# Hybrid decoder block on one core: x fetched ahead of the first scale block, column sums by products with ones, x turned a quarter at a time

## The chip, the core and the metric

The kernel runs on one core of a Trainium2 chip. The core has a matrix engine (TensorE, PE in the profile), a vector engine (VectorE, DVE), a scalar engine (ScalarE, ACT), a general engine (GpSimd, POOL) and a queue engine (SyncE, SP). All of them run their own instruction stream in order and wait for each other by semaphores; loads and stores are issued by SP, POOL and ACT and carried by 16 DMA engines. The metric is the device time of one execution in microseconds (us), the median of several runs.

## The reference

The input x has 512 positions by 2048 channels in float32. The part that matters here is the beginning:

```
mod = silu(c) @ w_ada + b_ada                     # c: 2048 values; w_ada: 2048 x 12288
shift1, scale1, gate1, shift2, scale2, gate2 = split(mod, 6)
h    = rms_norm(x, norm1_w) * (1 + scale1) + shift1
proj = h @ w_in                                   # w_in: 2048 x 7168, seven parts of 1024
attn = dilated_attention(q, k, v of proj)         # 8 heads
hg   = hgrn2(q, f, i, g of proj)                  # 8 heads of a gated recurrence
x    = x + gate1 * (concat(attn, hg) @ w_out)
x    = x + gate2 * (square(relu(h2 @ w_ff1)) @ w_ff2)   # h2: as h, with scale2 and shift2
```

Each sixth of mod needs 2048 x 2048 values of w_ada, 16.8 MB, to make 2048 numbers.

## The kernel before

Channels lie on the 128 partitions, 16 chunks k of 128 channels. The vector-matrix product for mod runs on VectorE: a block of columns of w_ada is loaded chunk by chunk (`araw`), and each chunk is multiplied by its 128 values of silu(c) and added to one of two running sums (`acc`, lines 127 and 129; one such instruction is called a multiply-add below). For scale1 a block has 256 columns: 8 loads of 256 KB and 16 multiply-adds. That gives the factors g1c of two chunks, so there are 8 scale blocks, and block p serves chunks 2p and 2p+1, called pair p. For shift1 and the others a block has 512 columns and 16 loads. The sums over the partitions are made by turning the sums on TensorE (`to_cols`, line 149) and adding along the row on ScalarE (line 152); two small VectorE operations (lines 167 and 169) add the bias and multiply by norm1_w.

x is loaded in 16 tiles `xs` (4 tiles of positions by 4 quarters of channels, line 255). ScalarE squares 14 of them and VectorE 2; the norm factor rx is ready after a power on GpSimd (line 212). The tiles are multiplied by rx (2 on ScalarE, 14 on VectorE, lines 277 and 279), turned on TensorE four at a time (line 283) and copied out (line 285), giving `xnT[k]`. For each chunk, `scaled` multiplies xnT[k] by g1c in place (line 335), rounds it into `hi` (line 336, ScalarE) and keeps the rest in `lo` (line 337, VectorE). Weights are treated likewise: `whi` (line 39, ScalarE) and `wlo` (line 40, VectorE), four buffers of each. A product is three TensorE products, hi by whi, lo by whi, hi by wlo.

`first_groups` (called once with scale1 alone, group 1, and once again, group 2) makes 512 + 256 columns of w_in: for each pair it takes 36 products of 128 x 512. The shift is added later, as a column made by another vector-matrix product (`shift_through`): its first one ends with an addition at line 143, is turned at line 149, and stands in TensorE's order inside the third projection, after 660 products of 128 x 512. The shift blocks, their columns and the first gate block are background steps (`bgw`), taken from within group 2.

The order of the instructions is set by a scheduler at build time, which puts them on each engine by its own estimate of when they can run; `issue_after` adds an order on one engine, and from the third projection on TensorE's order is the written one. At run time each engine follows its list. All loads of the first part stand in SP's list.

Of the kernel before, what the change touches and what calls it, by code (L numbers as in the profile page):

```python
# [15 lines left out]
P = 128  # L16
# [28 lines left out]
def hybrid_block(ctx, tc, x, c, positions, norm1_w, w_ada, b_ada, w_in, q_norm_w, k_norm_w,  # L45
# [29 lines left out]
    pool.memset(mhalf, -0.5)  # L75
# [10 lines left out]
    dve.tensor_copy(bcol, ps_c[:, 2 * NK:P])  # L86
    sc = const.tile([P, NK], F32, name="sc")
# [28 lines left out]
    def gemv(view, vec, col0, n=512, early=False):  # L116
# [3 lines left out]
        for k0 in range(0, NK, nk):  # L120
            raw = spare.pop(0) if early and spare else slot("araw") if early else gv.tile([P, 512], F32, name="araw", bufs=4)
            raw = raw.rearrange("p (k n) -> p k n", n=n)
            nc.sync.dma_start(raw, view[:, k0:k0 + nk, col0:col0 + n])
            for k in range(k0, k0 + nk):
                acc = accs[k % 2]
                if k < 2:
                    dve.tensor_scalar(acc, raw[:, k - k0], vec[:, k:k + 1], None, op0=ALU.mult)
                else:
                    dve.scalar_tensor_tensor(acc, raw[:, k - k0], vec[:, k:k + 1], acc, op0=ALU.mult, op1=ALU.add)  # L129
# [8 lines left out]
    def to_cols(accs, dst):  # L138

        nb = accs[0].shape[1] // P  # L140
        parts = 1 if nb == 4 else 2
        if parts == 1:
            dve.tensor_tensor(accs[0], accs[0], accs[1], op=ALU.add)
        yield
        pc = bank("pc")
        for j in range(nb):
            for u in range(parts):
                c = (j * parts + u) * P
                pe.transpose(pc[:, c:c + P], accs[u][:, j * P:(j + 1) * P], ident)
        for j in range(nb):  # L150
            c = pc[:, j * parts * P:(j + 1) * parts * P]
            act.activation(c, c, AF.Copy, accum_out=dst[:, j:j + 1])
# [7 lines left out]
    def mod_cols(kind, b, dst, nw, n=512, early=False):  # L160

        for _ in gemv(ada_v, sc, kind * D + b * n, n, early):
            yield
        nb = n // P
# [3 lines left out]
        if nw is not None:  # L168
            mod_cols.last = dve.scalar_tensor_tensor(d, d, 1.0, nw[:, b * nb:(b + 1) * nb], op0=ALU.add, op1=ALU.mult)
# [16 lines left out]
    def load_w(view, k0, c0, n=512, eng=None, ahead=True, raws=None):  # L186
        with tc.high_priority() if ahead else ExitStack():
            raw = wr.tile([P, 2, n], F32, name="wraw", tag="raw", bufs=4)
            nc.sync.dma_start(raw, view[:, k0:k0 + 2, c0:c0 + n])
# [20 lines left out]
    def rstd_of(dst, ss, n, inv_n):  # L210
        dve.tensor_scalar(dst, ss, inv_n, EPS, op0=ALU.mult, op1=ALU.add)
        pool.tensor_tensor(dst, dst, mhalf[:, 0:n], op=ALU.pow)
# [34 lines left out]
    first_scale = mod_cols(1, 0, g1c, n1c, 256, True)  # L247
    for _ in range(8):
        next(first_scale)
# [1170 lines left out]
```

## Time and profile before

| what | value |
|---|---|
| runs (median; all) | 2300.57 us; 2303.32, 2300.57, 2293.37 |
| the profiled execution | 2297.95 us, span in the profile 2296.2 us, mean granted TensorE clock 0.996 |
| busy in the span | PE 2224.9 us (97%), DVE 1809.9 (79%), ACT 1098.2 (48%), POOL 447.3 (19%) |
| first 128 x 512 product of the kernel | at 36.80 us |
| moved by DMA | 598.31 MB, mean 261 GB/s |

Times are counted from the start of the span. A row of the timeline has start, duration, engine, line, operation, out<-in with sizes, a count where equal instructions follow each other, and in brackets how long the engine had been idle and what ended it. The duration of an instruction includes its tail; where many follow each other, the pace is the distance of their starts, which is shorter. A row of the waits has who waited for whom, the total, the number of times and the longest. A row of the windows has, for a stretch, the busy time of PE, weight loads, DVE, ACT and POOL with counts, the granted clock, the DMA engines' share and GB/s.

### The profile page before, as it was taken

How to read it: one execution, taken by the hardware profiler on the slowest of the kernel's cores; microseconds unless marked ns; L12 is line 12 of the kernel's file. 1: busy time of each engine (PE TensorE's matmuls, PEld its weight loads, DVE VectorE, ACT ScalarE, POOL GpSimd, SP SyncE). 2: the span in 40 equal slices, each digit the busy share in tenths (PEclk: the TensorE clock that was granted, in tenths of full speed). 3: DMA queues.
4: the chain of work that ended last, by engine and by line, in shares of the span. 5: the costliest groups of instructions: out<-in, count | busy, mean ns of one | idle time of the engine just before them, and what ended most of it. 6: DMA issues, size and time to landing. Idle time of an engine off the chain costs nothing.

```text
span 2296.2 us, 33105 instructions
## 1 busy us (share of the span) xinstructions
PE 2224.9 (97%) x11769; PEld 1824.4 (79%) x11769; DVE 1809.9 (79%) x2765; ACT 1098.2 (48%) x1950; POOL 447.3 (19%) x664
## 2 busy tenths in 40 slices
PE   4899999999999999999999999999999999999999
PEld 3787877888778888778887888888888888888887
DVE  6999777677876565668648988988897679967878
ACT  5555434433344454447544556555564333343332
POOL 1000022000230000002232323323332222222221
PEclk9999999999999999999999999999999999999999
DMA  9798455556545256746969799889889987998784
GB/s 327 254 335 315 124 177 156 177 160 207 187 151 184 68 173 225 247 152 217 367 231 383 251 344 347 298 306 386 298 328 390 339 293 260 385 344 291 278 301 164
DMA packets 262582, 598.31 MB, mean 261 GB/s; under 512 B 23220, under 2 KB 43968, under 8 KB 262416
## 3 DMA queue, kind: packets, MB, share of 16 engines
q1 hardware_dynamic: 186800, 332.54, 43.1%
q0 software_dynamic: 70720, 254.21, 30.0%
q10 hardware_dynamic: 4896, 9.44, 1.2%
q8 instruction: 93, 1.52, 0.3%
q14 instruction: 73, 0.60, 0.1%
HBM read 518.49 MB, written 77.61 MB: 260 GB/s over the span
## 4 chain that ended last, share of the span: by engine, by line
PE 60%; DVE 17%; DMA 14%; issue 6%; ACT 2%; POOL 1%; SPq 0%; DVEq 0%; ACTq 0%; POOLq 0%
PE f L1177 9%; PE f L1178 9%; PE f L1176 9%; DMA araw<-in_w_ada_dram 6%; PE prj L198 5%; PE prj L199 5%; PE prj L200 5%; DVE vlo L1161 3%; DVE acc L129 3%; DVE raw L1144 2%; PE f L208 2%; PE f L206 2%; PE f L207 2%; DMA Fl<-f_lod 2%; DVE wlo L40 2%
## 5 line engine op out<-in xcount | busy, mean ns | idle before, releaser
L1160 ACT CAST vhi<-raw 128x1024 fp32r<-128x1024 f32 x392 | 413.4, 1055 | 534.5 <-PE f L1178 416.3
L1161 DVE TENSOR_TENSOR vlo<-raw,vhi 128x1024 fp32r<-128x1024 f32 x392 | 475.5, 1219 | 153.5 <-ACT vhi L1160 152.7
L1177 PE MATMUL f<-vlo,Fh 128*128 128x512 f32 x1376 | 537.1, 390 | 3.9 <-DVE vlo L1161 3.8
L1178 PE MATMUL f<-vhi,Fl 128*128 128x512 f32 x1376 | 535.8, 389 | 0.8 <-DMA Fl<-f_lod 0.8
L1176 PE MATMUL f<-vhi,Fh 128*128 128x512 f32 x1376 | 536.1, 390 | 0.0
L39 ACT CAST whi<-wraw 128x512 fp32r<-128x512 f32 (+1 forms) x368 | 219.8, 601 | 453.2 <-PE prj L200 313.3
L198 PE MATMUL prj<-whi,hi 128*128 128x512 f32 x896 | 364.9, 407 | 1.3 <-ACT gg L701 1.3
L200 PE MATMUL prj<-whi,lo 128*128 128x512 f32 x896 | 351.4, 392 | 0.0
L199 PE MATMUL prj<-wlo,hi 128*128 128x512 f32 x896 | 351.0, 392 | 0.0
L40 DVE TENSOR_TENSOR wlo<-wraw,whi 128x512 fp32r<-128x512 f32 (+1 forms) x368 | 243.2, 665 | 120.9 <-ACT whi L39 118.3
L129 DVE SCALAR_TENSOR_TENSOR acc<-araw,sc,acc 128x512 f32<-128x512 f32 (+1 forms) x392 | 252.7, 672 | 100.5 <-DMA araw<-in_w_ada_dram 99.2
L1177 PEld LDWEIGHTS f<-vlo,Fh 128*128 128x128 f32 x1376 | 258.3, 188 | 63.3 <-DVE vlo L1161 10.0
L1178 PEld LDWEIGHTS f<-vhi,Fl 128*128 128x128 f32 x1376 | 258.3, 188 | 54.8 <-DMA Fl<-f_lod 1.6
L1176 PEld LDWEIGHTS f<-vhi,Fh 128*128 128x128 f32 x1376 | 258.3, 188 | 53.5
L1144 DVE TENSOR_TENSOR raw<-raw,raw 128x1024 f32<-128x1024 f32 x224 | 267.7, 1216 | 4.1 <-DMA raw<-in_w_ff_dram 3.9
L198 PEld LDWEIGHTS prj<-whi,hi 128*128 128x128 f32 x896 | 169.3, 189 | 36.5 <-ACT gg L701 1.6
L200 PEld LDWEIGHTS prj<-whi,lo 128*128 128x128 f32 x896 | 168.9, 188 | 36.7
L199 PEld LDWEIGHTS prj<-wlo,hi 128*128 128x128 f32 x896 | 169.5, 189 | 33.0 <-DVE wlo L40 1.0
L1122 POOL DMA_DIRECT2D Fh<-f_hid x112 | 79.0, 705 | 425.9 <-PE f L1178 410.8
L208 PE MATMUL f<-hi,wlo 128*128 128x512 f32 x256 | 99.8, 390 | 1.3 <-DVE wlo L40 1.3
L206 PE MATMUL f<-hi,whi 128*128 128x512 f32 x256 | 100.2, 391 | 0.0
L207 PE MATMUL f<-lo,whi 128*128 128x512 f32 x256 | 99.6, 389 | 0.0
(311 smaller groups left out, 2917.0 us busy)
## 6 DMA issues: line engine op xcount, KB each, us to landing
raw<-in_w_ff_dram SPq DMA_DIRECT2D x224, 512.0 KB, 9.7
araw<-in_w_ada_dram SPq DMA_DIRECT2D x384, 256.0 KB, 4.3
Fh<-f_hid POOLq DMA_DIRECT2D x112, 512.0 KB, 6.5
Fl<-f_lod POOLq DMA_DIRECT2D x112, 512.0 KB, 7.7
wraw<-in_w_in_dram SPq DMA_DIRECT2D x104, 512.0 KB, 4.1
Fh<-h_hid POOLq DMA_DIRECT2D x60, 512.0 KB, 6.6
Fl<-h_lod POOLq DMA_DIRECT2D x60, 512.0 KB, 7.5
f_hid<-part POOLq DMA_DIRECT2D x48, 512.0 KB, 7.9
```

The lines of the kernel that those rows point to most:

```text
L39: nc.scalar.copy(hi, src)
L40: (eng or nc.vector).tensor_tensor(lo, src, hi.bitcast(F32), op=ALU.subtract)
L129: dve.scalar_tensor_tensor(acc, raw[:, k - k0], vec[:, k:k + 1], acc, op0=ALU.mult, op1=ALU.add)
L198: pe.matmul(banks[ti], lhsT=hi[:, ts], rhs=whi, start=first, stop=False)
L199: pe.matmul(banks[ti], lhsT=hi[:, ts], rhs=wlo, start=False, stop=False)
L200: pe.matmul(banks[ti], lhsT=lo[:, ts], rhs=whi, start=False, stop=last)
L1144: dve.tensor_tensor(dst, a, b, op=ALU.subtract)
L1160: act.copy(hi, src)
L1161: split_done.append(dve.tensor_tensor(lo, src, hi.bitcast(F32), op=ALU.subtract))
L1176: pe.matmul(banks[t], lhsT=fh[u][a][:, ts], rhs=whi[:, a], start=first, stop=False)
L1177: pe.matmul(banks[t], lhsT=fh[u][a][:, ts], rhs=wlo[:, a], start=False, stop=False)
L1178: pe.matmul(banks[t], lhsT=fl[u][a][:, ts], rhs=whi[:, a], start=False, stop=end)
```

## The change

Six things are changed, all before the third projection:

1. The 16 loads of x are issued first; the 8 loads of scale block 0 follow, then the first pair's weights, then the other 56 loads of the scale blocks in a row. Before, scale block 0 was ahead of x, and weights and scale loads alternated.
2. The weights of group 1 (from pair 1 on) and of group 2 are issued by POOL instead of SP.
3. The squares are shared 8 to 8 between ScalarE and VectorE (14 to 2 before), the multiplications by rx 8 to 8 (2 to 14 before).
4. A scale block's sums over the partitions are two products with a column of ones for each chunk (`L188` in the new file), and one ScalarE instruction applies norm1_w and a bias prepared at the start (`L191`). The turning, the adding along rows and the two VectorE operations go.
5. x is turned a quarter at a time: quarter 0 before scale block 0 is summed, each other quarter inside the loop over pairs. `scaled` makes hi first and the scaled xnT after it.
6. `behind` fixes the order of the steps on each engine: a block's multiply-adds come after the block ahead and, except the first four, after the last `lo` of the pair that this block's forerunner serves.

The instruction lists of the changed kernel differ as follows (order of issue only; no times). VectorE, around the place where scale block 2 ends and chunks 4 and 5 are split; acc is a running sum, wlo the rest of a weight tile, lo the rest of a chunk, g1c the scale factors. Before:

```order
L127 TENSOR_SCALAR acc<-araw,sc 128x256 x2
L129 SCALAR_TENSOR_TENSOR acc<-araw,sc,acc 128x256
L169 SCALAR_TENSOR_TENSOR g1c<-g1c,n1c 128x2
L129 SCALAR_TENSOR_TENSOR acc<-araw,sc,acc 128x256 x8
L337 TENSOR_TENSOR lo_687<-xnT,hi_686 128x512
L129 SCALAR_TENSOR_TENSOR acc<-araw,sc,acc 128x256 x2
L40 TENSOR_TENSOR wlo<-wraw,whi 128x512
```

Now:

```order
L133 SCALAR_TENSOR_TENSOR acc<-araw,sc,acc 128x256 x2
L40 TENSOR_TENSOR wlo<-wraw,whi 128x256
L133 SCALAR_TENSOR_TENSOR acc<-araw,sc,acc 128x256
L337 TENSOR_TENSOR lo_618<-xnT,hi_617 128x512
L337 TENSOR_TENSOR lo_623<-xnT,hi_622 128x512
L312 TENSOR_SCALAR xs<-xs,rx 128x512 x2
L131 TENSOR_SCALAR acc<-araw,sc 128x256 x2
L40 TENSOR_TENSOR wlo<-wraw,whi 128x512
L133 SCALAR_TENSOR_TENSOR acc<-araw,sc,acc 128x256 x2
L40 TENSOR_TENSOR wlo<-wraw,whi 128x512
```

Before, multiply-adds of the next block stand between the end of a block and the chunk's `lo`; now the chunk's `lo` follows directly on the block's last multiply-add, and the next block's come behind it.

ScalarE at the same place in the changed kernel (xnT copies are turned quarters of x on their way out of PSUM, hi the rounded chunks, whi the rounded weights):

```order
L320 COPY xnT<-ptx 128x512
L191 ACTIVATE g1c<-pc,bcol,n1c 128x1 x2
L335 ACTIVATE hi_617<-xnT,g1c 128x512
L320 COPY xnT<-ptx 128x512
L335 ACTIVATE hi_622<-xnT,g1c 128x512
L336 ACTIVATE xnT<-xnT,g1c 128x512
L320 COPY xnT<-ptx 128x512
L336 ACTIVATE xnT<-xnT,g1c 128x512
```

`lo_618` reads the first of the two L336 results, so five ScalarE instructions stand between the sums and it.

The diff, cut to its core:

```diff
+    ones = mhalf[:, 16:17]
...
+    b1c = bcol[:, NK:2 * NK]
+    dve.scalar_tensor_tensor(b1c, b1c, 1.0, n1c, op0=ALU.add, op1=ALU.mult)
...
-    def to_cols(accs, dst):
...
-        nb = accs[0].shape[1] // P
-        parts = 1 if nb == 4 else 2
...
+    def to_cols(accs, dst, lag=1):
+
+        dve.tensor_tensor(accs[0], accs[0], accs[1], op=ALU.add)
+        for _ in range(lag):
+            yield
         pc = bank("pc")
...
+    def scale_cols(b):
+
+        steps = gemv(ada_v, sc, D + b * 256, 256, True)
+        for _ in range(NK // 2):
+            with ExitStack() as order:
+                for ins in scale_cols.behind:
+                    order.enter_context(tc.issue_after(ins))
+                next(steps)
+            yield
+        next(steps, None)
+        scale_cols.behind = [gemv.last.ins, gemv.load.ins]
+        accs = gemv.acc
+        scale_cols.last_dve = gemv.last
+        pc = bank("pc")
+        for j in range(2):
+            for u in range(2):
+                pe.matmul(pc[:, j:j + 1], lhsT=accs[u][:, j * P:(j + 1) * P], rhs=ones, start=u == 0, stop=u == 1)
+        for j in range(2):
+            ks = slice(2 * b + j, 2 * b + j + 1)
+            scale_cols.last = act.activation(g1c[:, ks], pc[:, j:j + 1], AF.Identity, scale=n1c[:, ks],
+                                             bias=b1c[:, ks])
+        yield
...
-    first_scale = mod_cols(1, 0, g1c, n1c, 256, True)
-    for _ in range(8):
-        next(first_scale)
...
-                if q == 3 and ti % 2:
+                if ti % 2:
...
+    def x_turned(k, *anchors):
+
+        q, j = k // 4, k % 4
+        if j == 0:
+            for ti in range(NT):
+                if ti % 2:
+                    with tc.issue_after(anchors[0].ins):
+                        x_turned.dve = dve.tensor_scalar(xs[ti][q], xs[ti][q], rx[:, ti:ti + 1], None, op0=ALU.mult)
+                else:
+                    with tc.issue_after(anchors[1].ins):
+                        x_turned.act = act.activation(xs[ti][q], xs[ti][q], AF.Copy, scale=rx[:, ti:ti + 1])
+        pt = bank("ptx")
+        for ti in range(NT):
+            x_turned.pe = pe.transpose(pt[:, ti * P:(ti + 1) * P], xs[ti][q][:, j * P:(j + 1) * P], ident)
+        t = slot("xnT")
+        act.copy(t, pt)
+        xnT.append(t)
...
+    def pair_of_weights(k0, c_f, c_q, queue):
+        return (load_w(win_v, k0, c_f, ahead=False, queue=queue),
+                load_w(win_v, k0, c_q, 256, None, ahead=False, queue=queue))
+
+    def scaled(k):
+        for l, t in zip((hhi, hlo), pair(k)):
+            l.append(t)
+        act.activation(hhi[k], xnT[k], AF.Copy, scale=g1c[:, k:k + 1])
+        a = act.activation(xnT[k], xnT[k], AF.Copy, scale=g1c[:, k:k + 1])
+        scaled.last = dve.tensor_tensor(hlo[k], xnT[k], hhi[k].bitcast(F32), op=ALU.subtract), a
...
-            wt = load_w(win_v, k0, c_f, ahead=False)
-            wc = load_w(win_v, k0, c_q, 256, None, ahead=False)
+            with tc.issue_after(rx_ready.ins):
+                wt, wc = first_weights.pop() if first_weights else pair_of_weights(k0, c_f, c_q, pool)
...
         elif k0 < 14:
-            run_all(mod_cols(1, k0 // 2 + 1, g1c, n1c, 256, True))
-        for k in (k0, k0 + 1):
-            scaled(k)
+            steps = scale_cols(k0 // 2 + 1)
+            for _ in range(2):
+                next(steps)
+        if k0:
+            for k in (k0, k0 + 1):
+                scaled(k)
+        if 0 < k0 < 14:
+            scale_cols.behind.append(scaled.last[0].ins)
+            run_all(steps)
+        for k in (range(4, 8), range(8, 12), range(12, 16), (), (), (), (), ())[k0 // 2]:
+            x_turned(k, *scaled.last)
...
-    later.insert(0, shift_through(4096 + 512))
+    later.insert(0, behind(shift_through(4096 + 512), gemv.load.ins))
```

More of the change, by code (lines that the diff above doesn't have):

```diff
@@ L128, in gemv @@
                 else:
-                    dve.scalar_tensor_tensor(acc, raw[:, k - k0], vec[:, k:k + 1], acc, op0=ALU.mult, op1=ALU.add)
+                    gemv.last = dve.scalar_tensor_tensor(acc, raw[:, k - k0], vec[:, k:k + 1], acc, op0=ALU.mult,
+                                                         op1=ALU.add)
             yield
@@ L158, in hybrid_block, with behind, mod_cols @@
     gcol = const.tile([P, NK], F32, name="gcol")
-    def mod_cols(kind, b, dst, nw, n=512, early=False):
-        for _ in gemv(ada_v, sc, kind * D + b * n, n, early):
-            yield
-        nb = n // P
+    def behind(steps, *anchors):
+        while True:
+            with ExitStack() as order:
+                for ins in anchors:
+                    order.enter_context(tc.issue_after(ins))
+                if next(steps, steps) is steps:
+                    return
+            yield
+    def scale_cols(b):
+        steps = gemv(ada_v, sc, D + b * 256, 256, True)
+        for _ in range(NK // 2):
+            with ExitStack() as order:
+                for ins in scale_cols.behind:
+                    order.enter_context(tc.issue_after(ins))
+                next(steps)
[13 more added lines that the diff above has]
+        yield
+    def mod_cols(kind, b, dst, nw, early=False):
+        for _ in gemv(ada_v, sc, kind * D + b * 512, 512, early):
+            yield
+        nb = 4
         d = dst[:, b * nb:(b + 1) * nb]
@@ new lines, in hybrid_block @@
+    scale_cols.behind = [rstd_of.mean.ins]
+    first_scale = scale_cols(0)
+    for _ in range(8):
+        next(first_scale)
+    xnT = []
+    def x_turned(k, *anchors):
[14 more added lines that the diff above has]
+        xnT.append(t)
@@ L269, in hybrid_block @@
+    scaled(0)
+    with tc.issue_after(scaled.last[1].ins), tc.issue_after(x_turned.dve.ins):
+        first_weights = [pair_of_weights(0, 4096, 3072, nc.sync)]
+    first_weights_load = load_w.last
+    scaled(1)
+    second_scale = scale_cols(1)
     spare.extend((hp0, hp1)[k % 2].tile([P, 512], F32, name="araw", tag=f"{c}{k}")
                  for k in range(8, NK) for c in ("hi", "lo"))
+    scale_cols.behind += [first_weights_load.ins, scaled.last[0].ins]
     for _ in range(8):
         next(second_scale)
-    xnT = []
@@ L274, in hybrid_block @@
-    for q in range(4):
-        for ti in range(NT):
-            if q == 0 and ti % 2 == 0:
-                act.activation(xs[ti][q], xs[ti][q], AF.Copy, scale=rx[:, ti:ti + 1])
-            else:
-                dve.tensor_scalar(xs[ti][q], xs[ti][q], rx[:, ti:ti + 1], None, op0=ALU.mult)
-        for j in range(4):
-            pt = bank("ptx")
-            for ti in range(NT):
-                pe.transpose(pt[:, ti * P:(ti + 1) * P], xs[ti][q][:, j * P:(j + 1) * P], ident)
-            t = slot("xnT")
-            act.copy(t, pt)
-            xnT.append(t)
@@ L327, in shift_block @@
             bg_step()
-        for k in [k for k in behind if k // 4 in shift_done]:
+        for k in [k for k in unshifted if k // 4 in shift_done]:
             shifted(k)
-            behind.remove(k)
-    def scaled(k):
-        for l, t in zip((hhi, hlo), pair(k)):
-            l.append(t)
-        act.activation(xnT[k], xnT[k], AF.Copy, scale=g1c[:, k:k + 1])
-        act.copy(hhi[k], xnT[k])
-        dve.tensor_tensor(hlo[k], xnT[k], hhi[k].bitcast(F32), op=ALU.subtract)
+            unshifted.remove(k)
     def shifted(k):
```

58 lines of the change are left out of this document (29 added, 29 removed).

## Prediction

> **What bounds the kernel now.** I read the waits of TensorE first, over the whole execution (who waited for whom: us in total, times, longest):
>
> ```profile
> PE ptx L283 <- ACT xs L277: 12.8, 1, 12.8
> PE pc L149 <- DVE acc L129: 12.4, 3, 11.4
> PE prj L206 <- ACT hi L336: 6.9, 3, 4.1
> PE pc L149 <- DVE acc L143: 4.9, 1, 4.9
> ```
>
> These four are the largest, and all lie in the part that is changed: x is not normed, the scale factors are late, and at 209 to 214 us TensorE waits for the sum of the first shift column (line 143). The windows (PE, weight loads, DVE, ACT, POOL busy; clock, DMA share, GB/s) say what stands behind the last one:
>
> ```profile
> 0.00:26.60 26.60, 1.74 (x5) 0.86 (x5) 8.90 (x25) 11.28 (x34) 8.43 (x23) 1.00 0.88 291
> 26.60:92.90 66.30, 55.35 (x268) 45.05 (x268) 65.98 (x170) 38.47 (x87) 1.21 (x1) 1.00 1.07 353
> 92.90:130.00 37.10, 35.80 (x149) 28.88 (x150) 28.39 (x82) 21.39 (x42) 4.75 (x8) 0.92 0.47 152
> 130.00:214.00 84.00, 79.30 (x355) 64.52 (x353) 83.36 (x145) 46.66 (x106) 0.53 (x1) 0.99 1.01 362
> 214.00:2296.00 2082.00, 2052.73 (x10994) 1685.10 (x10994) 1623.24 (x2346) 980.35 (x1682) 432.40 (x631) 1.00 0.73 255
> ```
>
> VectorE is busy 65.98 of 66.30 us and 83.36 of 84.00 us: from 26.6 us to that sum it is the bound, idle only 0.32 + 8.71 + 0.64 = 9.7 us. Behind 214 us TensorE is busy 98.6% and its work is not edited, so a shift of that sum shifts the end. The question is thus when VectorE ends line 143 in the changed kernel. Its row, and the ones around x:
>
> ```profile
> 2.11 5.37 SPq L123 DMA_DIRECT2D araw<-in_w_ada_dram  x8
> 7.52 13.09 SPq L255 DMA_DIRECT2D xs<-in_x_dram  x16
> ...
> 13.30 2.46 DVE L129 SCALAR_TENSOR_TENSOR acc<-araw,sc,acc 128x256 f32<-128x256 f32 x6 [0.91 <-DMA araw<-in_w_ada_dram]
> ...
> 25.12 0.63 ACT L264 ACTIVATE jk<-xs 128x512 f32<-128x512 f32 x1 [0.49 <-DMA xs<-in_x_dram]
> ...
> 26.62 0.35 DVE L127 TENSOR_SCALAR acc<-araw,sc 128x256 f32<-128x256 f32 x1
> ...
> 27.23 0.16 DVE L211 TENSOR_SCALAR rx<-rx 128x4 f32<-128x4 f32 x1
> ...
> 27.48 1.21 POOL L212 TENSOR_TENSOR rx<-rx,mhalf 128x4 f32<-128x4 f32 x1 [14.29 <-DVE rx L211]
> ...
> 213.43 0.68 DVE L143 TENSOR_TENSOR acc<-acc 128x512 f32<-128x512 f32 x1
> ```
>
> x is complete at 25.1 us, VectorE's unbroken work starts at 26.6, block 0 was done before, in the wait for x. Line 143 ends at 214.0.
>
> **The change, part by part.** Rows that give the paces (distance of starts):
>
> ```profile
> 48.73 0.15 DVE L167 TENSOR_TENSOR g1c<-g1c,bcol 128x2 f32<-128x2 f32 x1
> 48.80 0.61 DVE L127 TENSOR_SCALAR acc<-araw,sc 128x256 f32<-128x256 f32 x2
> 49.33 0.48 DVE L129 SCALAR_TENSOR_TENSOR acc<-araw,sc,acc 128x256 f32<-128x256 f32 x1
> ...
> 55.90 3.24 DVE L129 SCALAR_TENSOR_TENSOR acc<-araw,sc,acc 128x256 f32<-128x256 f32 x8
> 59.07 0.68 DVE L337 TENSOR_TENSOR lo<-xnT,hi 128x512 fp32r<-128x512 f32 x1
> 59.67 0.88 DVE L129 SCALAR_TENSOR_TENSOR acc<-araw,sc,acc 128x256 f32<-128x256 f32 x2
> ...
> 32.84 2.46 DVE L279 TENSOR_SCALAR xs<-xs,rx 128x512 f32<-128x512 f32 x6
> ...
> 202.46 4.72 DVE L129 SCALAR_TENSOR_TENSOR acc<-araw,s1c,acc 128x512 f32<-128x512 f32 x7
> 207.10 0.48 DVE L127 TENSOR_SCALAR acc<-araw,s1c 128x512 f32<-128x512 f32 x1
> ...
> 5.78 0.18 ACT L88 ACTIVATE sc<-ps_c 128x16 f32<-128x16 f32 x1
> 50.19 1.33 ACT L335 ACTIVATE xnT<-xnT,g1c 128x512 f32<-128x512 f32 x2
> 51.43 0.36 ACT L152 ACTIVATE pc<-pc 128x256 f32<-128x256 f32 x1
> ...
> 38.24 3.53 ACT L285 COPY xnT<-ptx 128x512 f32<-128x512 f32 x7
> ...
> 43.13 1.91 PE L283 MATMUL ptx<-ident,xs 128*128 128x128 f32 x16
> 49.91 0.60 PE L149 MATMUL pc<-ident,acc 128*128 128x128 f32 x4
> ```
>
> On VectorE a multiply-add of 256 columns takes 0.396 us (8 in 3.17), the first two of a block 0.265, so a block 6.1; one of 512 columns 0.66; `lo` and its like 0.60; a multiplication by rx 0.40; a small operation 0.07. On ScalarE a scaling takes 0.62, a copy out of PSUM 0.49; on TensorE a turning 0.115.
>
> *x first.* The 8 loads that go behind x are 2.1 MB, at 353 GB/s 5.9 us: x is complete at 19.2 instead of 25.1. The last square (0.69), the sum and the mean follow, and multiply-adds start at 20.3 instead of 26.6: a gain of 6.3 us. The power (1.21), the multiplications, 16 turnings and 4 copies of quarter 0 fit beside block 0's 6.1 us; without that cover the power and first two multiplications alone would add 2 us.
>
> *VectorE's work to that sum.* Before: 214.0 - 26.6 = 187.4, less 9.7 idle, 177.7 us. The instruction lists up to it are equal except: block 0 is no longer done in the wait (+6.1); 6 multiplications by rx move to ScalarE (-2.4); 14 small operations on g1c go (-1.0); of the first gate block 7 multiply-adds and an addition now stand behind the sum (-4.6 - 0.6). The six added squares run while x lands. 177.7 + 6.1 - 8.6 = 175.2, and 20.3 + 175.2 = 195.5. So the changed kernel may let VectorE idle 18.5 us and breaks even.
>
> *Idle time.* This is where the change costs. The list of VectorE shown above has `lo` right behind a block's last multiply-add. `lo` needs: the narrow products on TensorE, which the trace does not show (bounds: nothing, and twice the 0.45 us of four turnings; I take 0.45, the same weights being loaded); two g1c on ScalarE (bounds 0.1 and 0.36 by the 0.18 of line 88; I take 0.3); two `hi` and one scaled xnT at 0.62; tails and handovers 0.3, in all 2.9 us. A copy between adds 0.49. Behind the waiting `lo` all of the next block's multiply-adds are queued, but for four (1.3 us) in some blocks. By block: 0: 2.9. 1: 12 turnings and a copy more, four multiply-adds less: 2.9 + 1.4 + 0.5 - 1.3 = 3.5. 2: one copy ahead and one between, half a microsecond of it before the block's end, and 0.5 for the second `lo`: 4.0. 3: the same, and about 1.0 because a `wlo` stands ahead of the release of its `whi` by TensorE: 5.0. 4: 2.9 - 1.3 = 1.6. 5 and 6: two `wlo` more to fill, 1.0 each. Sum 19.0. Behind block 7 shift loads now follow the scale loads without a gap, so that the 8.71 us of 92.9 to 130 should mostly vanish; for that stretch and the many short handovers I take 3.5 (bounds: 0.64, and the 9.7 of before). 22.5 in all; with the bounds of its parts 14 to 31.
>
> 195.5 + 22.5 = 218.0 against 214.0: **4.0 us later**. All that the early x and the lighter VectorE gain, and a little more, goes into waits behind each block. The first product comes early (27.2 for block 0, then the chain, a second scaling and a weight cast: about 30.6 instead of 36.80), but that lead is used up by block 3.
>
> *TensorE's clock.* Rows with the idle time ahead of them:
>
> ```profile
> 52.47 1.21 PE L206 MATMUL prj<-hi,whi 128*128 128x512 f32 x4 [1.96 <-ACT hi L336]
> ...
> 94.20 2.08 PE L206 MATMUL prj<-hi,whi 128*128 128x512 f32 x4 [4.06 <-ACT hi L336]
> ...
> 214.17 1.11 PE L149 MATMUL pc<-ident,acc 128*128 128x128 f32 x4 [4.86 <-DVE acc L143]
> 214.94 0.78 PE L198 MATMUL prj<-whi,hi 128*128 128x512 f32 x1
> ...
> 217.64 0.63 PE L198 MATMUL prj<-whi,hi 128*128 128x512 f32 x1
> 218.07 0.63 PE L199 MATMUL prj<-wlo,hi 128*128 128x512 f32 x1
> ```
>
> After 1.96 us the products keep 0.23 us; after 4.06 and 4.86 they run at 0.43 for some 4 us, which costs 2.3 us. In the changed kernel block 7 ends at about 27.2 + 67.3 of VectorE's work + 21 idle = 115.5; 1.7 to the first product, 408 products at 0.2275 to the shift column, 3.8 for a `lo` behind eight multiply-adds and 0.9 of turnings make TensorE arrive at 214.7, 3.3 us ahead of the sum. That lies between the rows; a halved restart there would cost what it costs before. I take a third of it as saved, -0.8. A gap of about 5 us ahead of block 1's products restarts cold too; half of its 2.3 us reaches block 2's sums: +1. The Trainium skill, "TensorE: Matmul & The Clock Gate" (Part 1: The HAM clock gate), says that about 3.4 us without work halve the clock and about 3.4 us of work restore it. Both rows above agree; by that rule 3.3 us would just stay fast and the whole 2.3 would be saved, which moves the sum by 1.5 us.
>
> **The sum**, against the profiled execution: 2297.95 + 4.0 - 0.8 + 1.0 = 2302.2. The median of the runs is 2.6 above that execution, so a median of about 2304.
>
> **The rivals.** *VectorE keeps running (faster).* If the chain is short enough or the list leaves VectorE no more idle than the 9.7 of before, the sum comes at 205.2, 8.8 earlier: 2292 as a median. For it: VectorE idled 0.3 us in 66 before, with the same operations. Against: before, the next block's multiply-adds stood ahead of `lo`; now they stand behind. *The weights on POOL's queue come late (slower).* Landing times:
>
> ```profile
> wraw<-in_w_in_dram SPq DMA_DIRECT2D x104, 512.0 KB, 4.1
> Fl<-f_lod POOLq DMA_DIRECT2D x112, 512.0 KB, 7.7
> ```
>
> A weight buffer is free when `wlo` has read it, one pair (10 us or more) before it is needed, so 7.7 plus an issue is covered; from some 11 us on each pair waits. At 13.5 it is 2.5 us in six pairs, 15 us: 2319. The Trainium skill, "DMA: Bandwidth & Descriptors" (SWDGE vs HWDGE vs iDMA), says that descriptors of GpSimd's loads are written by GpSimd into SBUF and can be locked out by VectorE. No row here shows it; against it stands 7.7 with VectorE 79% busy. *The slow clock is paid in the loop.* Waits of 3 us and more ahead of blocks 1 to 4 and pair 7 each restart TensorE slowly, and where its end gates the next block's sums (blocks 4 to 6, where a pair's end and the next block's end coincide within 0.3 us) 2.3 us count: four times 2.3 on top, 2313. *x does not come earlier*, because the start of the DMA engines and not the queue sets it (291 GB/s in the first window): 6 us on top, 2310.
>
> **How the numbers follow.** The forecast has 0.61, the running VectorE 0.14, POOL's queue 0.08, the slow clock 0.12, the late x 0.05. Bounds of the idle time (14 to 31, so -8.5 to +8.5 around 22.5) and 5 us between runs give the forecast 2294 to 2314; to hold 8 in 10 over all cases 2290 to 2316. A measurement tells about 0.5%, 11.5 us, from no change: 2289 to 2312. Faster has most of the far side of the first rival, 0.10; slower has POOL's queue, half of the slow clock and the forecast's edge, 0.16; the same 0.74.
>
> **What would show it.** Right: first product near 31 us; VectorE idle ahead of L337 about 3 us in blocks 0 to 3, less in 4 to 6; 20 to 25 us idle in all up to the shift column's sum, at about 218; the 289th product near 130 instead of 122; no more than 4 us of wait at the shift column. Wrong: VectorE idle under 15 us; waits of `whi` for weights from POOL; x complete after 22 us; a clock under 0.9 in the windows of 40 to 110.

## The result, and the profile after

The changed kernel takes 2316.16 us (median of 5, 2314.21 to 2317.16) against 2300.57 us: 1.0066 times the time before, with an interval of 1.0048 to 1.0084. It is slower by 0.66%, some 15 us, more than the 0.5% that can be told from no change. The forecast was 2304, the range ended at 2316, and "no measurable change" had 0.74 of the chances, slower 0.16, so the likeliest case did not come. The profiled execution has a span of 2314.4 us and its own time of 2316.16 us; both stand 18.2 us above those of before.

The waits of VectorE up to 232 us in the changed kernel (us in total, times, longest; the largest row that concerns the blocks, and two others behind x):

```profile
DVE lo L337 <- ACT xnT L336: 24.3, 9, 5.3
...
DVE wlo L40 <- ACT whi L39: 2.7, 4, 1.8
DVE acc L133 <- DMA araw<-in_w_in_dram: 2.2, 3, 1.3
```

In the kernel before, from 26.6 to 214 us, no row of `lo` is among VectorE's waits; the largest there is

```profile
DVE wlo L40 <- ACT whi L39: 4.7, 7, 1.8
```

The windows of the changed kernel (stretch and length, then busy us of PE, weight loads, DVE, ACT and POOL, granted clock, DMA share, GB/s): from the end of the first wait of `lo` to 127.7 us, from there to the shift column's sum, and the whole stretch from the first multiply-add to that sum:

```profile
31.30:127.70 96.40, 82.14 (x360) 66.67 (x361) 73.12 (x173) 46.14 (x92) 11.30 (x16) 0.88 0.75 236
127.70:227.30 99.60, 94.53 (x423) 77.49 (x422) 95.73 (x193) 57.73 (x127) 13.53 (x22) 1.00 0.92 322
20.97:227.30 206.33, 181.48 (x806) 148.48 (x806) 175.82 (x383) 109.70 (x228) 27.42 (x40) 0.94 0.85 284
```

VectorE is busy 175.82 of 206.33 us, idle 30.5, where the kernel before was idle 9.7. 24.3 us of it stand ahead of the blocks' `lo`, as the timeline of VectorE shows (start, duration, then the idle time ahead and what ended it):

```profile
20.97 0.61 DVE L131 TENSOR_SCALAR acc<-araw,sc 128x256 f32<-128x256 f32 x2
...
31.32 0.69 DVE L337 TENSOR_TENSOR lo<-xnT,hi 128x512 fp32r<-128x512 f32 x1 [3.38 <-ACT xnT L336]
...
47.65 0.69 DVE L337 TENSOR_TENSOR lo<-xnT,hi 128x512 fp32r<-128x512 f32 x1 [3.68 <-ACT xnT L336]
...
60.90 0.69 DVE L337 TENSOR_TENSOR lo<-xnT,hi 128x512 fp32r<-128x512 f32 x1 [3.87 <-ACT xnT L336]
...
77.06 0.69 DVE L337 TENSOR_TENSOR lo<-xnT,hi 128x512 fp32r<-128x512 f32 x1 [5.31 <-ACT xnT L336]
...
92.66 1.30 DVE L337 TENSOR_TENSOR lo<-xnT,hi 128x512 fp32r<-128x512 f32 x2 [2.71 <-ACT xnT L336]
...
104.97 1.31 DVE L337 TENSOR_TENSOR lo<-xnT,hi 128x512 fp32r<-128x512 f32 x2 [2.61 <-ACT xnT L336]
...
116.14 1.30 DVE L337 TENSOR_TENSOR lo<-xnT,hi 128x512 fp32r<-128x512 f32 x2 [1.92 <-ACT xnT L336]
...
226.66 0.69 DVE L145 TENSOR_TENSOR acc<-acc 128x512 f32<-128x512 f32 x1
...
230.94 0.55 DVE L618 TENSOR_SCALAR f<-f,omlb,lb 128x512 f32<-128x512 f32 x1 [0.33 <-ACT f L617]
```

The last row is the marker used from here on: the first VectorE instruction on a forget tile (line 553 before, 618 after), the first work behind the shift column that both kernels have. It stood at 218.16 us and now stands at 230.94: 12.8 us later. What TensorE did at the same places:

```profile
23.03 3.67 PE L318 MATMUL ptx<-ident,xs 128*128 128x128 f32 x16 [18.82 <-ACT xs L315]
...
31.85 1.65 PE L241 MATMUL prj<-hi,whi 128*128 128x512 f32 x3 [3.02 <-ACT whi L39]
...
71.50 0.56 PE L188 MATMUL pc<-mhalf,acc 128*128 128x1 f32 x2 [2.71 <-DVE acc L133]
...
88.38 1.79 PE L188 MATMUL pc<-mhalf,acc 128*128 128x1 f32 x8 [2.73 <-DVE acc L133]
91.46 2.08 PE L241 MATMUL prj<-hi,whi 128*128 128x512 f32 x4 [1.29 <-ACT hi L335]
...
101.53 0.95 PE L188 MATMUL pc<-mhalf,acc 128*128 128x1 f32 x8
...
227.41 0.66 PE L151 MATMUL pc<-ident,acc 128*128 128x128 f32 x4 [3.60 <-DVE acc L145]
```

The first product is early as forecast (31.85, before 36.80). The eight narrow products with ones, unknown before, take 0.95 us at the full clock and 1.79 us at 88.38. That row is at half clock, and it is not the only such stretch. Windows cut at the edges of four of them (PEclk is the number behind POOL's count):

```profile
30.40:37.20 6.80, 5.35 (x13) 4.19 (x14) 5.88 (x14) 5.00 (x10) 1.44 (x2) 0.50 1.11 349
71.40:78.20 6.80, 6.71 (x26) 5.96 (x27) 1.08 (x3) 4.59 (x9) 0.00 (x0) 0.50 0.70 229
88.40:95.20 6.80, 5.51 (x17) 4.65 (x18) 4.08 (x11) 3.04 (x6) 0.00 (x0) 0.50 0.94 315
115.70:119.10 3.40, 3.40 (x9) 2.46 (x8) 2.96 (x7) 1.02 (x2) 0.00 (x0) 0.51 0.72 272
```

The kernel before has two of them ahead of its marker:

```profile
92.30:99.10 6.80, 4.90 (x11) 3.60 (x12) 6.80 (x15) 4.72 (x8) 0.00 (x0) 0.50 0.50 154
211.80:218.60 6.80, 4.43 (x13) 3.66 (x14) 6.40 (x11) 3.22 (x9) 0.00 (x0) 0.50 1.06 387
```

The trace holds the granted clock from its first change on, at 27.0 us in the changed kernel and at 34.3 in the kernel before; ahead of that change the windows print 1.00, and the pace has to be read instead. The 16 turnings from 23.03 us on take 3.67 us, while 20 of them take 2.34 at full clock in a run below, so TensorE began at half clock.

Against the forecast, step by step (us; the sum is the end of line 145, once 143):

| | forecast | measured | later by |
|---|---|---|---|
| multiply-adds start | 20.3 | 20.97 | 0.7 |
| VectorE's work to the sum | 175.2 | 175.8 | 0.6 |
| VectorE idle to the sum | 22.5 | 30.5 | 8.0 |
| sum of the shift column ends | 218.0 | 227.3 | 9.3 |

### The profile page after: what moved, and what is told of

The parts are those of the page before. It is cut to its first block, busy times and chain, and to the rows that moved or that the text cites. A ratio compares the mean times of both kernels' runs of the same rounds, so it can differ in the third digit from the quotient of the medians.

```text
span 2314.4 us, 33167 instructions
## 1 busy us (share of the span) xinstructions
PE 2236.6 (97%) x11801; PEld 1835.8 (79%) x11801; DVE 1810.4 (78%) x2756; ACT 1097.3 (47%) x1928; POOL 467.1 (20%) x695
## 4 chain that ended last, share of the span: by engine, by line
PE 69%; DVE 14%; DMA 10%; issue 4%; ACT 2%; SPq 0%; POOL 0%; DVEq 0%; ACTq 0%; POOLq 0%
PE f L1242 11%; PE f L1243 11%; PE f L1241 11%; PE prj L233 6%; PE prj L235 6%; PE prj L234 6%; DMA araw<-in_w_ada_dram 6%; DVE vlo L1226 3%; DVE acc L133 3%; PE f L243 2%; PE f L241 2%; PE f L242 2%; DVE raw L1209 2%; PE prj L242 1%; PE prj L243 1%
```

## The experiments

The question was why VectorE idles 30.5 us and not 9.7. The theories, by the letters that some expectations use: A, the waits behind the blocks are lost time one for one, and multiply-adds moved into them win it back. B, the order held on each in-order engine decides: a wait that is filled comes back at the next instruction that TensorE or ScalarE releases, unless that one is moved too. Beside these stood the clock (TensorE's halved stretches lie in the ring from sums to `lo`), POOL's queue, C (the parts of the change that shorten work are gains, and the loss lies in the order and in x's early place), D (x first is itself a loss) and E (what is won ahead of the shift column is lost later to waits and the clock). In macs_ahead, macs_ahead_splits_late and warm the order of TensorE's, VectorE's, ScalarE's and SP's instructions is a list that copies the changed kernel's, with only the named moves; each ratio is to the kernel before on the same chip.

**macs_ahead.** At least eight multiply-adds of the next block are put ahead of each block's `lo`; the two places in the code that keep them behind it go, and the list holds the new order:

```diff
-    scale_cols.behind += [first_weights_load.ins, scaled.last[0].ins]
+    scale_cols.behind += [first_weights_load.ins]
...
-            scale_cols.behind.append(scaled.last[0].ins)
```

> The changed kernel with the order of every engine held as it is, but on VectorE the first eight multiply-adds of each scale block stand ahead of the first lo of the block before (none or four do in the changed kernel). Theory A (the prediction's: the idle time ahead of lo is the loss, and work put into it is gained one for one): the wait ahead of line 337 falls from 24 us to about 10, the sum of the first shift column comes 12 us earlier, median about 2304. Theory B (the blocks hang on a ring VectorE, TensorE, ScalarE, and the weight splits that now follow earlier on VectorE wait for TensorE to release their buffers): the wait at line 337 falls to 6 to 10 us, but 8 us of new waits for weights (line 40) appear, and the time falls by 4 us only, 2312.

Measured: 2315.29, 1.0064 (1.0046 to 1.0081), the marker at 231.0. Nothing was won that can be told; VectorE's idle time up to the sum is 28.2 us instead of 30.5. VectorE's waits up to 232 us:

```profile
DVE wlo L40 <- ACT whi L39: 12.3, 12, 2.2
...
DVE lo L337 <- ACT xnT L336: 7.7, 8, 2.1
```

The wait of `lo` fell from 24.3 to 7.7 us, and that of the weight splits rose from 2.7 to 12.3. A falls: the time that was filled was not won. The mechanism is B's, but its number was too good as well.

**macs_ahead_splits_late.** The same, with nine multiply-adds ahead and each VectorE split of the weights (line 40) six multiply-adds later in the list. No other edit.

> As the run before, with nine multiply-adds ahead of lo, and each weight split (line 40) between the lo of block 1 and that of block 7 moved six multiply-adds later on VectorE, so that it does not wait for TensorE. Theory A: no better than the run before, 2304. Theory B: VectorE's idle time up to the first shift column's sum falls from 30 us to about 17, that sum comes at about 215 instead of 227, and the median is about 2304 where the run before has 2312; the two theories part at the difference of these two runs: nothing by A, 8 us by B.

Measured: 2305.53, 1.0018 (1.0005 to 1.0030), the marker at 221.7, so 9.2 us earlier than in the changed kernel. The sum stands at 218.2 and VectorE's idle time up to it is 20.9 us, where B expected 215 and 17. VectorE's waits, and the windows around the only half-clock stretch that the trace records ahead of the sum:

```profile
DVE lo L337 <- ACT xnT L336: 10.3, 8, 2.6
...
DVE wlo L40 <- ACT whi L39: 3.4, 3, 1.8
```

```profile
26.00:97.50 71.50, 60.57 (x287) 48.45 (x285) 56.39 (x134) 41.22 (x82) 8.03 (x11) 1.00 0.88 285
97.50:100.90 3.40, 3.17 (x8) 2.30 (x8) 3.40 (x9) 0.35 (x1) 0.70 (x1) 0.50 0.48 154
100.90:218.20 117.30, 111.41 (x503) 91.02 (x501) 111.52 (x229) 66.79 (x144) 16.18 (x26) 1.00 0.87 304
```

The 1.00 of the first window holds from 39.5 us on, the first change of the clock in this trace; before that the pace is that of half clock:

```profile
32.74 2.07 PE L241 MATMUL prj<-hi,whi 128*128 128x512 f32 x4 [3.02 <-ACT whi L39]
```

The first move alone gave nothing; with the second it gives about 10 us, as B expects of a single queue with two sorts of waits in it. This is the clearest of the differences to the changed kernel; the intervals lie far apart. Two things stay open: the second move was not tried without the first, and half clock fell too. Behind 42 us macs_ahead has 13.6 us of it (at 75.7, 89.4 and 116.7), this run 3.4. In the run `warm` below 13.6 us less of it go with 3.4 us less at the sum; at that price 2 to 3 of the 9.3 us between the two markers are the clock's (an estimate).

**order_free.** Of the order that the change adds, one line is taken out, and the scheduler places the multiply-adds from block 2 on:

```diff
-            scale_cols.behind.append(scaled.last[0].ins)
```

> The changed kernel without the line that queues a block's remaining multiply-adds behind the last lo of the pair (the scheduler chooses; it puts weight splits and multiply-adds in another order too). Theory A (the forced order alone is the loss): 2303. Theory B (multiply-adds ahead of lo only move the wait to the weight splits): the wait at lo halves, waits of 5 us and more for weights appear, the first shift column's sum comes 2 to 4 us earlier, 2312.

Measured: 1.0040 (1.0027 to 1.0053), 2303.81 beside 2294.6 for the kernel before on that chip; the sum at 222.7 (4.6 earlier), the marker at 226.3. `lo` waits 12.2 us instead of 24.3, and the splits 6.2 for ScalarE and 4.3 for TensorE. Of the 12.1 us that leave one wait, 7.8 enter the other (10.5 where there were 2.7). B expected the sum 2 to 4 us earlier. Against 2300.57, A's 2303 is +2 and B's 2312 is +11; by the ratio +9.2 was measured, nearer to B.

**warm.** In the order of the changed kernel, TensorE turns the identity into an unused part of the bank while it waits, so the computation is the same and TensorE has work that nobody reads:

```diff
-        for j in range(2):
-            for u in range(2):
-                pe.matmul(pc[:, j:j + 1], lhsT=accs[u][:, j * P:(j + 1) * P], rhs=ones, start=u == 0, stop=u == 1)
+        idle = [pe.transpose(pc[:, P:2 * P], ident, ident) for _ in range((0, 14, 0, 20, 20, 0, 0, 0)[b])]
+        sums = [pe.matmul(pc[:, j:j + 1], lhsT=accs[u][:, j * P:(j + 1) * P], rhs=ones, start=u == 0, stop=u == 1)
+                for j in range(2) for u in range(2)]
...
+        idle = [pe.transpose(pc[:, P:2 * P], ident, ident) for _ in range((18, 0, 0, 0, 4, 4, 4, 4)[b])]
```

> The changed kernel with the order of every engine held, and turnings of the identity (0.115 us each at full clock, their results are not used) put on TensorE where it waits in blocks 0, 1, 3 and 4 (18, 14, 20, 20), and four behind the column sums of blocks 4 to 7. They only keep TensorE busy. If the halved clock is part of the loss (theory: four windows of 3.4 or 6.8 us in the first 130 us, which the kernel before had once): the granted clock in 40 to 130 us rises from about 0.88 to 0.97 or more, the wait ahead of block 3's and 4's lo falls from 5.3 and 2.7 us to 3.9 and 1.9, and the first shift column's sum comes 3 us earlier, median 2313. If the clock does not matter because VectorE's queue sets the pace: no change, 2316 within 1.

Measured: 2310.6, 1.0043 (1.0028 to 1.0058); the sum at 224.0 (3.4 us earlier), the marker at 227.6. Behind 38 us the windows show one half-clock stretch of 3.4 us ahead of the sum, where the changed kernel has three, of 17.0 us together:

```profile
26.00:73.00 47.00, 42.54 (x227) 35.99 (x226) 34.53 (x82) 26.36 (x52) 5.79 (x8) 1.00 0.80 252
...
89.30:92.70 3.40, 3.40 (x11) 2.82 (x12) 1.69 (x4) 2.29 (x4) 0.00 (x0) 0.50 1.08 347
92.70:224.00 131.30, 123.92 (x565) 101.16 (x563) 124.10 (x260) 71.78 (x154) 17.65 (x27) 1.00 0.87 299
```

The 1.00 of the first window holds from 34.7 us on, the first change of the clock in this trace. The 18 turnings of block 0 ran at half clock, as the pace says beside that of the 20 at block 3:

```profile
30.54 4.10 PE L194 MATMUL pc<-ident 128*128 128x128 f32 x18 [0.69 <-ACT g1c L192]
...
69.58 2.34 PE L186 MATMUL pc<-ident 128*128 128x128 f32 x20
```

The waits ahead of block 3's and block 4's `lo` fell from 5.31 and 2.71 us to 4.08 and 2.06, close to the 3.9 and 1.9 expected, while block 0's rose from 3.38 to 4.08. So keeping TensorE at work in the loop is worth 3.4 us at the sum, with what the turnings cost taken off. The two ratios' intervals overlap a little (1.0048 to 1.0058), so the time alone does not settle it; the evidence is one trace of each. The wait of `lo` stays in the main: 23.0 us instead of 24.3.

**weights_on_sync.** The weights go back to SP's queue, all else as in the change:

```diff
-                wt, wc = first_weights.pop() if first_weights else pair_of_weights(k0, c_f, c_q, pool)
+                wt, wc = first_weights.pop() if first_weights else pair_of_weights(k0, c_f, c_q, nc.sync)
```

> The changed kernel with the weights of pairs 1 to 7 and of the second group issued by SyncE again, as before the change (the scheduler then moves some instructions too). If the weights on POOL's queue come late (a rival of the prediction): 10 us less, 2306. If not, as the trace of the changed kernel says, where no weight cast waits for a landing: within 4 us of 2316, with the scale loads behind weights on one queue making up for what is gained.

Measured: 2311.82, 1.0048 (1.0031 to 1.0065), not told apart from the change by time (4.2 us less by the ratio, just outside the 4 expected); the marker at 231.7, 0.7 us later. POOL's queue is not what costs: in the changed kernel no row of ScalarE's waits up to 232 us has a rounded weight waiting for a landing. The DMA issues of the changed kernel up to 130 us agree (count, KB each, median us from issue to landing):

```profile
wraw<-in_w_in_dram POOLq DMA_DIRECT2D x9, 512.0 KB, 5.8
wraw<-in_w_in_dram POOLq DMA_DIRECT2D x9, 256.0 KB, 5.1
```

Then the parts of the change that can stand alone in the kernel before.

**gate_behind_alone.** Only the first gate block's order:

```diff
-    later.insert(0, shift_through(4096 + 512))
+    later.insert(0, behind(shift_through(4096 + 512), gemv.load.ins))
```

> The kernel before with one part alone: the loads and multiply-adds of the first gate block stand behind the last shift block's loads, which takes seven multiply-adds and one addition (5.2 us) off VectorE ahead of the first shift column's sum. TensorE waits 4.9 us for that sum in the kernel before, so no more than that, and 1 to 2 us of the halved clock behind it, can come out. Theory C: 2 to 5 us earlier, 2296 to 2298. Rival (VectorE's work ahead of the sum does not set it, DMA does): 2300 to 2301.

Measured: 2297.12 beside 2298.43 for the kernel before on that chip, 0.9992 (0.9983 to 1.0001), the marker at 217.0, 1.2 us earlier. A gain at the edge of what can be told.

**sums_alone.** Only the narrow products with ones and the one ScalarE instruction (`scale_cols` without its order) in place of the turning and the sums along rows:

```diff
-            run_all(mod_cols(1, k0 // 2 + 1, g1c, n1c, 256, True))
+            run_all(scale_cols(k0 // 2 + 1))
```

> The kernel before with one part of the change alone: the scale columns are summed by products with ones on TensorE and finished by ScalarE with scale and bias, in place of turnings, two accumulating copies and two VectorE operations a block. Nothing else is moved and no order is forced. Theory C (the parts of the change that shorten work are gains, and the loss lies in the forced order and in x's early place): VectorE has 1.0 us less to do, and the block's chain is shorter, so the first shift column's sum comes 1 to 3 us earlier: 2298. Rival (the products with one column are themselves slow on TensorE and hold up the chain): 2301 to 2304.

Measured: 2307.82, 1.0044 (1.0031 to 1.0057), the marker at 222.1. Expected was a small gain, or at most 4 us of loss by the rival; it is a larger loss. The windows show three half-clock stretches between 36 and 224 us, where the kernel before had two:

```profile
73.00:79.80 6.80, 6.80 (x22) 5.64 (x21) 6.80 (x17) 3.46 (x7) 0.00 (x0) 0.50 1.09 353
113.90:120.70 6.80, 4.79 (x11) 3.84 (x12) 3.64 (x17) 2.46 (x4) 0.00 (x0) 0.50 0.04 14
216.30:223.10 6.80, 4.96 (x14) 4.10 (x15) 6.40 (x11) 3.74 (x11) 0.00 (x0) 0.50 1.05 386
```

In the second the DMA engines move 14 GB/s, so there is a hole in the loads at that place. I suspect the order that the scheduler made of the other instructions, since the products themselves save work; no run shows it.

**sums_and_gate.** Both parts together:

> The kernel before with these two parts together, no forced order, block 0 ahead of x, weights on SyncE. Theory C: VectorE has 6.2 us less ahead of the sum, the blocks end earlier, and TensorE comes early enough to use it: the sum 9 to 11 us earlier than before, about 2290, faster than both kernels. If TensorE's own 98 per cent from 214 us on and its arrival at 209 us bound it: 2296.

Measured: 2295.28, 0.9986 (0.9977 to 0.9995): faster than both kernels, if by 0.14% only. The marker stands at 210.2, 8.0 us earlier than before, and the sum comes 7.5 us earlier where C expected 9 to 11; the time gains 3.2 us only, which is the second case of the expectation (2296), not C's 2290. TensorE's waits between 230 and 720 us, and the window around the second of them:

```profile
PE pB L592 <- DVE z L619: 5.9, 3, 3.3
PE ptq L472 <- ACT p_sb L510: 3.7, 1, 3.7
```

```profile
460.00:476.00 16.00, 12.34 (x59) 10.36 (x58) 9.55 (x22) 10.99 (x25) 0.00 (x0) 0.79 0.33 98
```

The lead, the median shift of like instructions against the kernel before, shrinks from about 10 us at 400 to 3.5 at 700: waits of 2.3 to 3.7 us in the attention, each followed by a half-clock stretch (372, 468, 666 us). The profiled execution took 2298.73 us and was the slowest of the eleven, so it may show more loss than most.

**sums_gate_x_first.** The same, and x's loads ahead of scale block 0's:

```diff
-    first_scale = scale_cols(0)
-    for _ in range(8):
-        next(first_scale)
     xs = [[slot("xs") for _ in range(4)] for _ in range(NT)]
...
+    first_scale = scale_cols(0)
+    for _ in range(8):
+        next(first_scale)
```

> As the run before, with x fetched ahead of the first scale block as in the changed kernel (one more part). The prediction counted this part as a gain of 6.3 us in VectorE's start against 6.1 us of block 0 that no longer lies in the wait for x, so nothing: 2290 as the run before. Theory D (x first is a loss: block 0's chain now stands behind x's instead of beside its loads, so the first product and every block behind it comes later): 5 to 8 us slower than the run before, 2296.

Measured: 2301.96, 1.0012 (1.0001 to 1.0024), 6.7 us above the kernel that it differs from, on the same chip; the marker 7.8 us later (218.0). VectorE waits for block 0 instead of working on it while x lands:

```profile
20.42 0.61 DVE L131 TENSOR_SCALAR acc<-araw,sc 128x256 f32<-128x256 f32 x2 [14.22 <-DMA araw<-in_w_ada_dram]
...
29.66 0.16 DVE L283 TENSOR_REDUCE rx<-ssx 128x4 f32<-128x16 f32 x1
```

The gain that was to pay for it did not come in this kernel: without the change's order VectorE put its last two squares behind 14 of block 0's 16 multiply-adds, and the sum of the squares, at 20.69 in the changed kernel, came at 29.66. So this is the price of x first without the orders, not of x first as such. It shows something else too: the first product is at 39.2, 7.4 us later than in the changed kernel, yet `lo` of block 5 is at 91.8 and not at 104.97. The early start does not decide here; the waits in the loop weigh more.

**sums_gate_warm.** The faster kernel, with the identity turned on TensorE in the attention's waits (24 unused turnings in the first attention, 14 in each of the two recurrences), the order of VectorE and ScalarE behind 300 us held:

```diff
+                    for _ in range(24):
+                        pe.transpose(pt[:, 0:P], ident, ident)
...
+            for _ in range(14 if h == 3 and i else 0):
+                pe.transpose(pB_all[:, 2 * P:3 * P], ident, ident)
```

> The kernel with sums and gate part, with turnings of the identity (results not used) put on TensorE where it waits later: 24 ahead of the last head's second turning in the first attention (3.7 us of wait at 468 us), 14 ahead of the last head's second half of level products in each of the two recurrences (2.3 and 3.3 us at 371 and 665 us); the order of VectorE and ScalarE from 300 us on is held as in the kernel before. There the early lead of 9.3 us at 300 us shrinks to 3.5 at 700. Theory E (half of what is given back is the halved clock that these waits bring, 3.4, 6.8 and 3.4 us of it against 3.4 in the kernel before, each worth half its length): these three windows vanish, the lead at 700 us is 7 to 9 us, median 2290 to 2292. Rival (the lead is given back because VectorE and the loads set the time there, and the clock only fills their wait): the lead at 700 us stays 3 to 4, median 2295.

Measured: 2290.78 beside 2294.6 for the kernel before on that chip, 0.9986 (0.9974 to 0.9997). The three half-clock stretches between 230 and 720 us are gone, and the lead at 700 us is 7.0 us instead of 3.5, as E expected; at the end the ratio is the same as without. In the profiled execution the lead is lost between 900 and 2000 us, where nothing was edited; but that execution took 2299.09 us, the slowest of twelve and 8.3 us above their median, so its end says little of the others. Whether the attention's clock counts for the time remains open.

**x_turned_at_once.** The changed kernel with all of x turned ahead of the blocks:

```diff
-    for k in range(4):
+    for k in range(16):
         x_turned(k, sum_ready, last_square)
...
-        for k in (range(4, 8), range(8, 12), range(12, 16), (), (), (), (), ())[k0 // 2]:
-            x_turned(k, *scaled.last)
```

> The changed kernel with one part undone: all of x is multiplied by rx and turned ahead of the blocks, as in the kernel before, not by quarters in blocks 0 to 2. If turning by quarters helps (the first product comes early, 31.8 us): the first product at about 38 us and the time 3 to 6 us longer, 2320. If it costs (its turnings, copies and multiplications stand in the chain of blocks 1 to 3, and x holds the buffers that block 4's loads wait for): the first product at 38 us, but blocks 1 to 3 are 2 to 3 us shorter each, the first shift column's sum 6 to 9 us earlier, 2308.

Measured: 2308.02 beside 2294.6, 1.0052 (1.0040 to 1.0064); the first product at 39.3 instead of 31.85, the sum at 224.3, the marker at 228.2 (2.8 earlier). The first product is 7.5 us later and the end no later: the quarters' early start is worth nothing here, and putting turnings and copies into the chain behind each block costs about as much as it brings. By time alone the two are not told apart.

All runs together. The shift by time is (ratio - 1) x 2300; the marker's is from one profile each:

| kernel | ratio | by time, us | marker, us |
|---|---|---|---|
| the change | 1.0066 | +15.2 | +12.8 |
| macs_ahead | 1.0064 | +14.7 | +12.9 |
| macs_ahead_splits_late | 1.0018 | +4.1 | +3.6 |
| order_free | 1.0040 | +9.2 | +8.1 |
| warm | 1.0043 | +9.9 | +9.4 |
| weights_on_sync | 1.0048 | +11.0 | +13.5 |
| x_turned_at_once | 1.0052 | +12.0 | +10.0 |
| gate_behind_alone | 0.9992 | -1.8 | -1.2 |
| sums_alone | 1.0044 | +10.1 | +4.0 |
| sums_and_gate | 0.9986 | -3.2 | -8.0 |
| sums_gate_x_first | 1.0012 | +2.8 | -0.2 |
| sums_gate_warm | 0.9986 | -3.2 | -6.4 |

In ten of twelve the time follows the marker within 3.5 us, and the intervals of the ratios are 2 to 4 us to each side. Most of the loss of the change thus lies ahead of the shift column. The profiled execution lost a further 5.4 us behind it (12.8 at the marker, 18.2 at the end): against the kernel before, the median lag of like instructions grows from 12.5 us at 440 to 19.9 at 700, in the attention, and is about 17 from 1000 on. By the runs' medians (+15.2) only 2.4 of the 5.4 remain, within the interval, so whether they belong to the kernel or to the two executions is not shown. Added up step by step, sums and gate stand at -3.2, with x first on top at +2.8, and the rest of the change (quarters, the order, POOL's queue, the 8-to-8 sharing) brings it to +15.2. The sharing was not tried alone.

## Why the prediction was right or wrong

**Right in kind.** The forecast said that VectorE sets the shift column, that x would be early, that VectorE would have less to do, and that waits behind each block would eat both and more. All of that is in the trace: the start within 0.7 us, the work within 0.6, the first product within 1.3, the largest waits ahead of line 337. It also named 3.3 us of wait of TensorE at the shift column; 3.6 were measured, followed by a half-clock stretch of 3.4 us (before 6.8), so the small gain there (0.8 forecast) has the right sign: the marker moved 0.5 us less than the sum. That the wait came out so close is luck: TensorE arrived at 223.8 where 214.7 was forecast, and the sum was as late.

**The step that failed** is the term "idle time, 22.5 in all", which measured 30.5, just inside the upper bound given for it (31). It makes 8.0 of the 9.3 us by which the sum missed. Of the 8.0:

- Blocks 4 to 6: 1.6 + 1.0 + 1.0 = 3.6 forecast, 2.71 + 2.61 + 1.92 = 7.2 measured. What fills these waits was counted rightly: four multiply-adds of the next block stand ahead of `lo`, and two `wlo` more in blocks 5 and 6. The chain was counted too short. From the block's last multiply-add to `lo` the forecast took 2.9 us; 4.0, 5.1 and 3.9 were measured (88.63 to 92.66, 99.92 to 104.97, 112.23 to 116.14). At block 4 the narrow products run at half clock and take 1.79 us, where 0.45 was taken. At block 5 they start at 101.53 only, 1.6 us after the last multiply-add, as TensorE ends the pair before, and take 0.95; then ScalarE makes two g1c, two `hi` and the first scaled xnT, and `lo` starts at 104.97, 3.4 us after the narrow products. Block 6 has the same 3.4 us, and 0.5 us of the pair before ahead of them. ScalarE at block 5:

```profile
102.51 0.59 ACT L191 ACTIVATE g1c<-pc,bcol,n1c 128x1 f32<-128x1 f32 x2 [0.61 <-PE pc L188]
103.00 1.32 ACT L335 ACTIVATE hi<-xnT,g1c 128x512 fp32r<-128x512 f32 x2
104.22 1.33 ACT L336 ACTIVATE xnT<-xnT,g1c 128x512 f32<-128x512 f32 x2
```

- Blocks 0 to 3: 15.4 forecast, 17.1 measured (the 16.24 of the four rows above and two second `lo` with 0.40 and 0.41).
- Elsewhere: 3.5 forecast, 6.2 measured, mostly splits waiting for ScalarE (2.7) and multiply-adds waiting for loads (2.2).

**The clock** is in these numbers. The forecast put +1.0 us on half-clock products in the loop, and gave the rival "the slow clock is paid in the loop" 0.12 and a time of 2313, 3 us short of the result. That nearness is in part luck: the rival added four times 2.3 us, and taking away 13.6 of the 17.0 us of half clock behind 38 us won 3.4. A sign that the prediction had named for being wrong came with it, a clock under 0.9 in the windows of 40 to 110 us: it was 0.66 from 70 to 80 and 0.74 from 90 to 100. The 289th product, expected near 130 us, came at 137.4.

**The shift of the sum as shift of the end** held, with the marker in the sum's place, in ten of the twelve kernels within 3.5 us. In sums_alone it did not (4.0 at the marker, 10.1 by time), nor in sums_and_gate: of 8.0 us won, 3.2 were left. TensorE's 98.6% behind the shift column does not mean that a lead is kept; waits of a few microseconds for VectorE and ScalarE open in the attention.

**The other rivals.** VectorE that keeps running (0.14): no, 30.5 us idle. POOL's queue late (0.08): no, though its 2319 is as near to the result as the clock's 2313; the splits' 2.7 us are waits for ScalarE, not for loads, and SP's queue for the weights moved the marker 0.7 us the other way. x no earlier (0.05): no, the last square ends at 20.6. "x first" itself was counted as a gain of 6.3 against 6.1 us of block 0, so at nothing; the run without the orders lost 6.7, and how it stands with them was not measured alone.

The result lies at the very end of the range (2316.16 against 2316) and 12 us above the forecast: 3.4 us of loss were forecast and 15.6 measured. That it is no further out is owed to the width of the range. The forecast had taken the bounds of the idle time (14 to 31) as symmetric; every one of the terms left out (TensorE's place in the chain, half clock in the narrow products, weight splits that wait for ScalarE) pointed to the late side.

What stays open: why the narrow sums alone are slower, what the 8-to-8 sharing and the later weight splits do by themselves, how much of the gain of macs_ahead_splits_late is the clock's, and whether the attention's half-clock stretches cost time at the end.

## What to carry to other kernels

When an engine's list is held so that a waiting instruction is followed by all of the next block's work, count the whole chain to that instruction once for every block, from the moment at which the other engines can begin it, and let nothing fill it that stands behind it. Work moved into a wait may only move the wait to the next waiting instruction of the same list: here the first move alone gave nothing, both together about 10 us (the second alone was not tried). A lead won early in a program with one busy engine is not yet time won; look for the waits further on in which it can vanish.

## What the runs showed of the hardware

The clock was halved by shorter waits than expected. In the kernel before, 1.96 us of wait left it at full speed and 4.06 halved it; in the changed kernel 2.25 us (to 42.36) left it so. There, waits of 2.71 us (to 71.50) and 2.73 us (to 88.38) were each followed by half-clock stretches of 6.8 us, and 0.94 us of one-column products with 1.29 us of wait behind them (to 114.94) by one of 3.4 us at 115.7. The same two at block 5 (0.95 and 1.29, to 103.77) were followed by none, so the length alone does not decide. The starts lie on one grid of 3.41 us, and the lengths are one or two steps of it. The Trainium skill, "TensorE: Matmul & The Clock Gate" (Part 1: The HAM clock gate), says that activity is watched in free-running windows of 3413 ns and that an idle window, about 3.4 us, halves the clock. The grid agrees; the length of the wait does not, since 2.7 us do not fill such a window, and the measurement decides. By that rule the changed kernel would have had no half-clock stretch at 71 and 88 us.

Turnings count as work for the clock. In `warm` TensorE does little but 18 turnings of the identity from 30.54 to 34.3 us, 0.21 us apart at half clock, and the clock rises behind them at 34.7; with 20 more, 0.11 us apart, from 69.58 to 71.9 it stays at full speed, where the changed kernel falls to 0.50 at 71.4.
